# Recurrent gates as unsplit fp32 blocks in the quarters of the array, in a two-layer hybrid trunk

## The chip, the cores and the metric

The kernel is one program on one core of one Trainium2 chip. The metric is the device time of one execution in microseconds (us). Engines are named as in the profile: PE (TensorE matmul) and PEld (its weight loads), DVE (VectorE), ACT (ScalarE), POOL (GpSimd), SP (SyncE, which here issues all transfers).

## The reference

Two layers work on 1024 latent tokens and 256 context tokens, with 1024 features, in fp32. In each layer one input projection feeds two token mixers: attention, and a gated linear recurrence, which the change is about:

```python
def lru_coeffs(u, w_gates, b_gates, lam):            # for each direction d
    r = sigmoid(block_diag(u, w_gates[0]) + b_gates[0])   # 16 blocks of 64 x 64
    i = sigmoid(block_diag(u, w_gates[1]) + b_gates[1])
    log_a = -LRU_C * r * softplus(-lam)
    a = exp(log_a)
    b = sqrt(-expm1(2.0 * log_a)) * (i * u)
    return a, b
# h[t] = a[t] * h[t-1] + b[t], forward and backward, context before latent; y = h_fwd + h_bwd
# branch output: (y * silu(g_lru)) @ w_b_out
```

`u` is a slice of the projection after a centred depthwise convolution of width 4. Layer 1 needs no context outputs, so its branch gate is computed for the latent tokens alone.

## The kernel before

Features lie on the 128 partitions and tokens along the free axis, in three chunks: C (256 tokens), L0 and L1 (512 each). A projection tile is 128 output features: for each chunk 24 matmuls, since an fp32 product is made of three fp32r products of high and low parts (`gemm`, helper line L145). The high part of each weight half (`whi`, from `wraw`) is made on ACT (L226) or, where `weng[0]` is "g", on POOL (L224); the low part (`wlo`) on DVE (L227).

The recurrent stage comes after the q, k and v projections. It runs eight feature tiles t: a projection tile for `u` (evacuated by ACT into `up`), then one for the branch gate (`evac_g`: ACT takes a tanh from PSUM into `gbt`, DVE multiplies it with the same PSUM bank into `g2`, L876). When the last chunk of `u` is out, `conv` runs (one ACT, four DVE instructions), and DVE splits `uc` into `uh` and `ul`. The gate weights `gr` are block diagonal in a 128x128 square (two 64x64 blocks and zeros) and are split into `gh` (POOL) and `gl` (DVE). `gate` makes one gate of one chunk for one direction: three matmuls into one bank and an ACT tanh (L829) out of it, twelve times a tile. After the twelfth, `coeffs` puts out all that follows at once: per direction Exp, Tanh and Square on ACT (L844 to L846), two DVE products (L847, L848), Sqrt on ACT (L851), a POOL product (L853), the DVE scans in place over `ti` (L856; L858 and L860), and, per chunk, a POOL sum (L866), a DVE product with `g2` (L867) and the store `zb`.

What PE does, and in which order, is written out by hand: a list of events with due times in PE's planned time (`tl`); an event is run when the planned time of the matmuls put out so far passes it. For the other engines, the order of the program is a priority: an instruction takes its place in an engine's queue when its operands and buffers are ready in a planned run, and every queue then runs strictly in order. Nearly all tiles of the stage have a single buffer (`bufs=1`): `a1` of tile t+1 can't be written before the last reader of `a1` of tile t is done. PSUM has six banks under the tag "s" and two under "av"; projection chunks alternate between them, gates take "s". `mix` is a ring of four SBUF buffers shared by `up`, `c0` and `g2`.

After the eighth tile one more projection tile runs, then the events left over are drained, and attention begins with its loads of k, v and q, which stand behind the last `zb` stores on SP's queue.

Of the kernel before, what the change touches and what calls it, by code (L numbers as in the profile page):

```python
# [26 lines left out]
F32 = mybir.dt.float32  # L27
F32R = mybir.dt.float32r
AF = mybir.ActivationFunctionType
OP = mybir.AluOpType  # L30
# [6 lines left out]
CTX = 256  # L37
# [63 lines left out]
def trunk_kernel(ctx: ExitStack, tc: tile.TileContext, xT, cc, par, wmod, win, wgate, wo,  # L101
# [27 lines left out]
    def mix(name):  # L129
        return ring.tile([128, 1286], F32, name=name, tag="mix", bufs=4)  # L130
# [19 lines left out]


    par_sb = const.tile([128, DEPTH, PW], F32, name="par")
    DMA.dma_start(par_sb, par)
    cc_sb = const.tile([128, KT, 2], F32, name="cc")
    DMA.dma_start(cc_sb, cc)
    ones = const.tile([128, 1], F32, name="ones")
# [33 lines left out]


    sp4, hgb = {}, {}

    def recurrent_consts(l):
        lam = p(l, "lam", 0, 16)
# [513 lines left out]
    for l in range(DEPTH):  # L709
# [5 lines left out]
        with tc.tile_pool(name="qk", bufs=2, reuse_waits="tile") as work:  # L715
# [12 lines left out]
            def load_wv(i, k):  # L728
                wvr = sm("wvr")
                DMA.dma_start(wvr, win[l, V0 + i][:, 512 * k:512 * k + 512])  # L730
                cs_ = slice(i * 128, (i + 1) * 128)

                def f():
                    split(wvh[:, 4 * k:4 * k + 4, cs_], wvl[:, 4 * k:4 * k + 4, cs_],
                          wvr.rearrange("p (k n) -> p k n", k=4), "g", "v")
                tl.at(3.0, f)

            for i in range(2):
                for k in range(2):
                    tl.at(30.0 + 10.0 * (2 * i + k), lambda i=i, k=k: load_wv(i, k))  # L740
            tl.at(20.0, lambda: recurrent_consts(l))
            tl.fill(first)
            for g in groups[1:]:
# [26 lines left out]


        use_banks("g", "av")
        weng[0] = "g"
        with tc.tile_pool(name="lru", bufs=1, reuse_waits="tile") as work:
            sp = sp4[l]

            class Lru:
                def __init__(self, t):
                    self.t, self.left = t, len(ALL)
                    self.gr = work.tile([128, 4, 128], F32, name="gr", bufs=1)  # L780
                    DMA.dma_start(self.gr, wgate[l, t])
                    self.gh = work.tile([128, 4, 128], F32R, name="gh", bufs=2)
                    self.gl = work.tile([128, 4, 128], F32R, name="gl", bufs=2)
                    split(self.gh, self.gl, self.gr, "g", "v")
                    self.up = mix("up")
                    G.memset(self.up[:, 0:2], 0.0)
                    G.memset(self.up[:, 258:261], 0.0)
                    G.memset(self.up[:, 1285:1286], 0.0)
                    self.g2 = None
# [12 lines left out]
                def conv(self):  # L802
                    t, up = self.t, self.up
                    cw = [p(l, "conv_w", j * 8 + t) for j in range(4)]
                    c0 = mix("c0")[:, 0:1283]
                    S.activation(c0, up[:, 0:1283], AF.Identity, scale=cw[0], bias=p(l, "conv_b", t))
                    V.scalar_tensor_tensor(c0, up[:, 1:1284], cw[1], c0, op0=OP.mult, op1=OP.add)
                    V.scalar_tensor_tensor(c0, up[:, 2:1285], cw[2], c0, op0=OP.mult, op1=OP.add)
                    uc = self.uc = self.wt("uc", 2)
                    V.scalar_tensor_tensor(uc[:, 0:256], up[:, 3:259], cw[3], c0[:, 0:256],  # L810
                                           op0=OP.mult, op1=OP.add)
                    V.scalar_tensor_tensor(uc[:, 256:], up[:, 262:1286], cw[3], c0[:, 259:1283],
                                           op0=OP.mult, op1=OP.add)
                    self.uh, self.ul = self.wt("uh", dt=F32R), self.wt("ul", dt=F32R)
                    split(self.uh, self.ul, uc)
                    self.tg = [[self.wt(f"tr{d}"), self.wt(f"ti{d}")] for d in range(2)]
                    self.todo = [(d, gi, c) for d in range(2) for gi in range(2) for c in ("C", "L0", "L1")]
                    tl.at(28.0 if last else 36.0, self.gate)

                def gate(self):  # L820
                    d, gi, c = self.todo.pop(0)
                    dg = 2 * d + gi
                    off, n = CH[c]
                    ps = ptile("s", "gtps")
                    gh, gl, uh, ul = self.gh, self.gl, self.uh, self.ul
                    mm(ps[:, :n], gh[:, dg], uh[:, off:off + n], True, False)
                    mm(ps[:, :n], gh[:, dg], ul[:, off:off + n], False, False)
                    mm(ps[:, :n], gl[:, dg], uh[:, off:off + n], False, True)
                    S.activation(self.tg[d][gi][:, off:off + n], ps[:, :n], AF.Tanh, scale=0.5,  # L829
                                 bias=hgb[l][:, dg * 8 + self.t:dg * 8 + self.t + 1])  # L830
                    if self.todo:
                        tl.at(0.9, self.gate)
                    else:
                        self.coeffs()

                def coeffs(self):
                    t = self.t
                    co = []
                    for d in range(2):
                        s4 = sp[:, 0, d * 8 + t:d * 8 + t + 1]  # L840
                        s4n = sp[:, 1, d * 8 + t:d * 8 + t + 1]
                        tr_, ti = self.tg[d]
                        a, a2 = self.wt(f"a{d}"), self.wt(f"b{d}")
                        S.activation(a, tr_, AF.Exp, scale=s4n, bias=s4n)  # L844
                        S.activation(tr_, tr_, AF.Tanh, scale=s4, bias=s4)
                        S.activation(a2, a, AF.Square)  # L846
                        V.scalar_tensor_tensor(a2, a2, 1.0, tr_, op0=OP.add, op1=OP.mult)  # L847
                        V.scalar_tensor_tensor(ti, ti, 1.0, self.uc, op0=OP.add, op1=OP.mult)  # L848
                        co.append((a, a2, ti))
                    for a, a2, ti in co:  # L850
                        S.activation(a2, a2, AF.Sqrt, scale=0.25)  # L851
                    for d, (a, a2, ti) in enumerate(co):
                        G.tensor_mul(a2, a2, ti)  # L853
                        h = ti
                        if d == 0:
                            V.tensor_tensor_scan(h, a, a2, 0.0, op0=OP.mult, op1=OP.add)  # L856
                        else:
                            V.tensor_tensor_scan(h[:, 0:256][:, ::-1], a[:, 0:256][:, ::-1],  # L858
                                                 a2[:, 0:256][:, ::-1], 0.0, op0=OP.mult, op1=OP.add)
                            V.tensor_tensor_scan(h[:, 256:][:, ::-1], a[:, 256:][:, ::-1],  # L860
                                                 a2[:, 256:][:, ::-1], h[:, 0:1], op0=OP.mult, op1=OP.add)
                    for c in och:
                        off, n = CH[c]
                        y = self.g2[:, off:off + n]
                        s = co[0][2][:, off:off + n]
                        G.tensor_add(s, s, co[1][2][:, off:off + n])  # L866
                        V.scalar_tensor_tensor(y, s, 0.5, y, op0=OP.mult, op1=OP.mult)  # L867
                        DMA.dma_start(dd["zb"][t, c], y)

                def evac_g(self, c, ps):  # L870
                    off, n = CH[c]
                    if self.g2 is None:
                        self.g2 = mix("g2")
                    th = sm("gbt")
                    S.activation(th[:, :n], ps[:, :n], AF.Tanh, scale=0.5)
                    tl.at(0.9, lambda: V.scalar_tensor_tensor(  # L876
                        self.g2[:, off:off + n], th[:, :n], 1.0, ps[:, :n], op0=OP.add, op1=OP.mult))

            for t in range(8):
                u = Lru(t)  # L880
# [31 lines left out]


        use_banks("g")
        weng[0] = "a"
        with tc.tile_pool(name="att", bufs=2, reuse_waits="tile") as work:
            kv = {}

# [418 lines left out]
```

## Time and profile before

| | us |
|---|---|
| median of 3 runs (3193.29 to 3196.1) | 3194.48 |
| the profiled execution: its own time | 3197.96 |
| the profiled execution: span of the core | 3196.2 |
| recurrent stage of layer 0 (234 to 592): length, PE busy | 358, 343.6 |
| recurrent stage of layer 1 (1925 to 2250): length, PE busy | 325, 302.8 |
| granted PE clock, mean over the span | 0.986 |

The profile is that of one execution. "Busy" is the union of an engine's instructions. Matmuls overlap in their pipeline, so the duration of one (0.39 us) is longer than the distance from its start to the next one's start, and that distance is what it costs. An idle time is put down to the instruction that released the engine.

### The profile page before, as it was taken

The numbers are of one execution on the slowest core, as the hardware profiler recorded it, in microseconds if no ns is written. First come the engines' busy times: TensorE is split into PE (matmuls) and PEld (weight loads), VectorE is DVE, ScalarE is ACT, GpSimd is POOL, SyncE is SP. The second block draws the span as 40 slices with busy tenths as digits, with TensorE's granted clock in tenths as the row PEclk, the third lists the DMA queues.
The fourth block names the chain that finished last, engine by engine and source line by source line (L and its number), as shares of the span: only waits on it lengthen the run. The fifth ranks groups of instructions, "written<-read, shape, count | busy, mean of one in ns | idle before, by whom it ended". The sixth has DMA issues, their size and how long they took to land. (4 is left out here: it accounts for less than half of the span.)

```text
span 3196.2 us, 42921 instructions
## 1 busy us (share of the span) xinstructions
PE 3059.7 (96%) x14880; PEld 2430.8 (76%) x14880; DVE 2457.1 (77%) x3675; ACT 1749.6 (55%) x3060; POOL 1020.0 (32%) x777
## 2 busy tenths in 40 slices
PE   7999999999999999999899999899999999999999
PEld 3788788777777777787778778777777777777887
DVE  7665887589898988556685785997799999996544
ACT  4323667466666666545555324676477766673222
POOL 0211444234434333234432121433244444441000
PEclk9999999999999999999999999999999999999999
DMA  5443111311222122264555452111412121115554
GB/s 196 144 152 121 50 50 62 115 59 59 73 64 78 60 64 64 87 195 153 172 191 168 147 166 87 60 47 53 121 56 75 58 75 58 52 59 170 181 177 138
DMA packets 233049, 331.95 MB, mean 104 GB/s; under 512 B 53296, under 2 KB 99184, under 8 KB 232576
## 3 DMA queue, kind: packets, MB, share of 16 engines
q1 hardware_dynamic: 232832, 329.21, 32.0%
q8 instruction: 117, 1.92, 0.2%
q14 instruction: 100, 0.82, 0.1%
HBM read 252.54 MB, written 76.58 MB: 103 GB/s over the span
## 5 line engine op out<-in xcount | busy, mean ns | idle before, releaser
L145 PE MATMUL gps<-h,whi 128*128 128x512 f32 x3328 | 1041.4, 394 | 21.1 <-DVE g L876 15.3
L145 PEld LDWEIGHTS gps<-h,whi 128*128 128x128 f32 x3328 | 612.1, 190 | 148.4 <-issue 10.7
L1004 DVE TENSOR_TENSOR pl<-pf,ph 128x512 fp32r<-128x512 f32 x656 | 630.2, 961 | 83.1 <-ACT ph L1003 79.5
L145 PE MATMUL gps<-h,wlo 128*128 128x512 f32 x1664 | 654.5, 393 | 1.3 <-DVE wlo L227 1.3
L1002 ACT ACTIVATE pf<-s2ps 128x512 f32<-128x512 f32 x656 | 392.8, 599 | 348.1 <-issue 157.0
L1018 POOL TENSOR_TENSOR acc<-pf 128x512 f32<-128x512 f32 x256 | 352.0, 1375 | 713.1 <-ACT pf L1002 711.5
L980 DVE TENSOR_REDUCE mp<-s1ps 128x1 f32<-128x512 f32 (+1 forms) x800 | 454.1, 583 | 63.7 <-PE s1ps L145 60.8
L1003 ACT ACTIVATE ph<-s2ps 128x512 fp32r<-128x512 f32 x656 | 390.0, 595 | 0.0
L227 DVE TENSOR_TENSOR wlo<-wraw,whi 128x512 fp32r<-128x512 f32 x392 | 335.3, 878 | 61.4 <-ACT whi L226 32.7
L226 ACT ACTIVATE whi<-wraw 128x512 fp32r<-128x512 f32 x324 | 193.6, 627 | 333.8 <-PE gps L145 258.1
L145 PEld LDWEIGHTS gps<-h,wlo 128*128 128x128 f32 x1664 | 314.3, 189 | 69.9 <-DVE wlo L227 2.0
L145 PE MATMUL s1ps<-k,qa 128*128 128x512 f32 (+1 forms) x800 | 284.9, 363 | 12.3 <-DMA qa<-q0L 10.3
L145 PE MATMUL avps<-ph,vv 128*128 128x512 f32 x656 | 266.9, 407 | 0.0
L145 PE MATMUL avps<-pl,vv 128*128 128x512 f32 x656 | 260.2, 397 | 5.0 <-DVE pl L1004 4.9
L145 PE MATMUL s2ps<-qa,k 128*128 128x512 f32 x656 | 261.1, 398 | 1.8 <-DVE mp L980 1.6
L145 PE MATMUL s2ps<-qb,k 65*128 65x512 f32 x656 | 260.3, 397 | 0.0
L145 PE MATMUL gps<-e,whi 128*128 128x512 f32 x768 | 243.9, 399 | 0.2 <-DVE e L227 0.2
L360 POOL TENSOR_TENSOR macc<-macc,wmt 128x512 f32<-128x512 f32 x112 | 156.2, 1395 | 255.2 <-ACT wmt L358 221.9
L145 PE MATMUL qps<-h,whi 128*128 128x512 f32 x640 | 203.0, 398 | 1.5 <-DVE h L674 0.9
L1020 POOL TENSOR_TENSOR acc<-acc,pf 128x512 f32<-128x512 f32 x128 | 181.5, 1418 | 71.4 <-ACT pf L1002 69.2
L145 PE MATMUL gps<-c,whi 128*128 128x256 f32 x1024 | 197.2, 288 | 3.1 <-DVE c L222 2.1
L145 PEld LDWEIGHTS s1ps<-k,qa 128*128 128x128 f32 x800 | 151.6, 190 | 51.8 <-issue 6.4
(216 smaller groups left out, 5026.6 us busy)
## 6 DMA issues: line engine op xcount, KB each, us to landing
wraw<-in_win_dram SPq DMA_DIRECT2D x200, 256.0 KB
wraw<-in_wo_dram SPq DMA_DIRECT2D x192, 256.0 KB
wm<-in_wmod_dram SPq DMA_DIRECT2D x32, 512.0 KB
wm<-in_wmod_dram SPq DMA_DIRECT2D x8, 1024.0 KB
rb<-rq SPq DMA_DIRECT2D x64, 128.0 KB
k<-k SPq DMA_DIRECT2D x24, 320.0 KB
v<-vst SPq DMA_DIRECT2D x20, 256.0 KB
vv<-v SPq DMA_DIRECT2D x8, 640.0 KB
```

The source lines that it names most:

```text
L145: nc.tensor.matmul(o, a, b, start=start, stop=stop)
L226: S.activation(dst_hi, src, AF.Copy)
L227: (V if lo_eng == "v" else G).tensor_sub(dst_lo, src, r32(dst_hi))
L360: G.tensor_add(acc, acc, t)
L980: tl.at(0.3, lambda: V.reduce_max(self.mp[:, j, b:b + 1], ps[:, :n], axis=AX.X))
L1002: S.activation(pf, ps, AF.Exp)
L1003: S.activation(ph, ps, AF.Exp)
L1004: tl.at(1.4, lambda: V.tensor_sub(pl, pf, r32(ph)))
L1018: G.tensor_add(self.acc_tile(x), first, pf)
L1020: G.tensor_add(self.accs[x], self.accs[x], pf)
```

## The change

- The two 64x64 blocks of a gate tile are loaded unsplit (`gw`), without the zeros. Each gate of a chunk is made of two plain fp32 matmuls with 64 rows and 64 columns. Direction 0 puts block h on the partitions of half h, direction 1 on those of the other half, so the four matmuls of one gate of both directions use the four quarters of the array and write two banks. `gate` makes all four gates of a chunk in one visit (eight matmuls, four banks, four tanh), three visits a tile.
- Everything of direction 1 therefore stands with the two halves of the partitions swapped. `exchange` (two transfers, SBUF to SBUF) makes a swapped copy `us` of `uc`, and swaps the result of the backward scan back, into `a1`, before the sum. The parameters of direction 1 are loaded swapped (`recurrent_params`, five small transfers).
- `uh`, `ul`, `gh`, `gl` and their splits are gone. The first gate is due 24 (layer 1: 20) after the convolution instead of 36 (28).
- `coeffs` is cut into thirteen events with due times, direction 1 first; the merge is due 4 after the exchange.
- `evac_g`: ACT takes both the tanh and a copy out of PSUM (`th`, `g2`); one DVE product per tile joins them later, from SBUF.
- `weng[0]` stays "a": in the recurrent stage the high parts of weights are made on ACT instead of POOL. `c0` has a buffer of its own.

```diff
+    def recurrent_params():
+        DMA.dma_start(par_sb[:, :, lam_c:lam_c + 8], par[:, :, lam_c:lam_c + 8])
+        for a, n in ((gate_c + 16, 16), (lam_c + 8, 8)):
+            for h in range(2):
+                DMA.dma_start(par_sb[64 * h:64 * h + 64, :, a:a + n], par[64 - 64 * h:128 - 64 * h, :, a:a + n])
...
-        weng[0] = "g"
...
-                    split(self.gh, self.gl, self.gr, "g", "v")
+                    self.gw = work.tile([128, 4, 64], F32, name="gw", bufs=2)
+                    for h in (slice(0, 64), slice(64, 128)):
+                        DMA.dma_start(self.gw[h], wgate[l, t][h, :, h])
...
-                    c0 = mix("c0")[:, 0:1283]
+                    c0 = work.tile([128, 1283], F32, name="c0", tag="c0")
...
-                    split(self.uh, self.ul, uc)
+                    self.us = self.exchange(uc, self.wt("us"))
...
-                    tl.at(28.0 if last else 36.0, self.gate)
+                    self.todo = ["C", "L0", "L1"]
+                    tl.at(20.0 if last else 24.0, self.gate)
+
+                def exchange(self, a, b):
+                    DMA.dma_start(b[0:64], a[64:128])
+                    DMA.dma_start(b[64:128], a[0:64])
+                    return b
...
-                    mm(ps[:, :n], gh[:, dg], uh[:, off:off + n], True, False)
-                    mm(ps[:, :n], gh[:, dg], ul[:, off:off + n], False, False)
-                    mm(ps[:, :n], gl[:, dg], uh[:, off:off + n], False, True)
...
+                    ps = [ptile("s", "gtps") for _ in range(4)]
+                    for gi in range(2):
+                        for h in range(2):
+                            rows = slice(64 * h, 64 * h + 64)
+                            for d in range(2):
+                                o = 64 * (h ^ d)
+                                mm(ps[2 * gi + d][o:o + 64, :n], self.gw[rows, 2 * d + gi], self.uc[rows, off:off + n],
+                                   True, True, 0.03 + 0.245 * n / 512)
+                    for gi in range(2):
+                        for d in range(2):
+                            dg = 2 * d + gi
+                            S.activation(self.tg[d][gi][:, off:off + n], ps[2 * gi + d][:, :n], AF.Tanh, scale=0.5,
+                                         bias=hgb[l][:, dg * 8 + self.t:dg * 8 + self.t + 1])
                     if self.todo:
-                        tl.at(0.9, self.gate)
+                        tl.at(3.6, self.gate)
                     else:
-                        self.coeffs()
+                        tl.at(0.5, self.coeffs)
...
+                    for at, fn, *d in ((0, decay, 1), (0.5, gated, 1), (2, gated, 0), (4.5, decay, 0), (5, square, 1),
+                                       (9.5, square, 0), (11, root), (14, product, 1), (17, product, 0),
+                                       (17.5, scan, 1), (21.5, scan, 0), (22, self.exchange, i1, a1), (26, merge)):
+                        tl.at(at, lambda fn=fn, d=d: fn(*d))
...
-                    th = sm("gbt")
-                    S.activation(th[:, :n], ps[:, :n], AF.Tanh, scale=0.5)
-                    tl.at(0.9, lambda: V.scalar_tensor_tensor(
-                        self.g2[:, off:off + n], th[:, :n], 1.0, ps[:, :n], op0=OP.add, op1=OP.mult))
+                        self.g2, self.th = mix("g2"), self.wt("th")
+                    g2, th = self.g2, self.th
+                    S.activation(th[:, off:off + n], ps[:, :n], AF.Tanh, scale=0.5)
+                    S.activation(g2[:, off:off + n], ps[:, :n], AF.Copy)
+                    if c == och[-1]:
+                        a = 0 if "C" in och else CTX
+                        tl.at(2.5, lambda: V.scalar_tensor_tensor(g2[:, a:TOK], th[:, a:], 1.0, g2[:, a:TOK],
+                                                                  op0=OP.add, op1=OP.mult))
...
```

In the events, `decay` is Exp, Tanh and Square of one direction, `gated` and `square` the two DVE products, `root` both Sqrt, `product` the POOL product, `scan` the scan (two for direction 1), `merge` the sums, the products with `g2` and the stores.

## Rows read from the trace of the kernel before

**Rows 1.** The page: busy time of each engine, and the chain's shares by engine.
```profile
PE 3059.7 (96%) x14880; PEld 2430.8 (76%) x14880; DVE 2457.1 (77%) x3675; ACT 1749.6 (55%) x3060; POOL 1020.0 (32%) x777
PE 31%; DVE 7%; issue 3%; ACT 1%; POOL 1%; DMA 0%; SPq 0%; DVEq 0%; POOLq 0%; ACTq 0%
```

**Rows 2.** Windows: one tile's period of layer 0, then the sum of six of layer 1.
```profile
core 0: us, PE busy (x) PEld busy (x) DVE busy (x) ACT busy (x) POOL busy (x), PEclk, DMA share, GB/s
446.10:482.80 36.70, 35.14 (x182) 29.84 (x181) 30.93 (x25) 26.20 (x31) 17.47 (x14) 1.00 0.16 54
...
sum 205.40, PE 187.63 PEld 155.67 DVE 188.98 ACT 140.75 POOL 82.33; mean PE 31.27 PEld 25.94 DVE 31.50 ACT 23.46 POOL 13.72
```

**Rows 3.** TensorE's waits, us in total, times, longest: layer 0, then layer 1.
```profile
PE gps L145 <- DVE g L876: 7.9, 7, 2.1
PE gtps L145 <- ACT ti L829: 4.8, 3, 3.0
...
PE gtps L145 <- DVE g L876: 11.7, 3, 5.2
PE gps L145 <- DVE g L876: 7.4, 4, 2.9
```

**Rows 4.** Timeline of TensorE: two matmuls of a gate.
```profile
start us, us, engine line op out<-in xcount [idle before <-releaser]
446.30 0.39 PE L145 MATMUL gtps<-uh,gl 128*128 128x512 f32 x1
446.53 0.40 PE L145 MATMUL gtps<-uh,gh 128*128 128x512 f32 x1
```

**Rows 5.** Same columns: the softmax sums (lps) between other matmuls.
```profile
2303.64 0.28 PE L145 MATMUL s1ps<-k,qa 128*128 128x256 f32 x1
2303.85 1.06 PE L145 MATMUL lps<-acc,ones 128*32 128x512 f32 x8
2305.18 0.39 PE L145 MATMUL avps<-pl,vv 128*128 128x512 f32 x1
```

**Rows 6.** Groups of instructions, shapes kept apart: busy us, mean ns, idle before.
```profile
L226 ACT ACTIVATE whi<-wraw 128x512 fp32r<-128x512 f32 x324 | 193.6, 627 | 333.8 <-PE gps L145 258.1 <-issue 35.5 <-PE qps L145 19.4
L145 PE MATMUL lps<-acc,ones 128*32 128x512 f32 x544 | 76.6, 604 | 9.6 <-DVE mp L980 9.4
L829 ACT ACTIVATE tr<-gtps,hgb 128x512 f32<-128x512 f32 x64 | 42.8, 696 | 13.1 <-PE gtps L145 13.0
L227 DVE TENSOR_TENSOR ul<-uc,uh 128x1280 fp32r<-128x1280 f32 x16 | 24.1, 1508 | 0.0
L227 DVE TENSOR_TENSOR gl<-gr,gh 128x512 fp32r<-128x512 f32 x16 | 23.6, 1474 | 17.5 <-POOL gh L224 17.5
L875 ACT ACTIVATE gbt<-gps 128x512 f32<-128x512 f32 x32 | 18.8, 597 | 18.8 <-PE gps L145 18.7
L222 DVE CAST uh<-uc 128x1280 fp32r<-128x1280 f32 x16 | 16.1, 1006 | 0.1
```

**Rows 7.** Timelines: coefficients of a layer 1 tile; last, a scan of layer 0.
```profile
2071.87 0.47 ACT L829 ACTIVATE ti<-gtps,hgb 128x256 f32<-128x256 f32 x1 [3.03 <-DVE g L867]
2088.10 2.45 ACT L851 ACTIVATE b<-b 128x1280 f32<-128x1280 f32 x2
...
2090.58 6.75 POOL L853 TENSOR_TENSOR b<-b,ti 128x1280 f32<-128x1280 f32 x2
...
2094.43 5.58 DVE L856 TENSOR_TENSOR_SCAN ti<-a,b 128x1280 f32<-128x1280 f32 x1
2104.44 2.79 DVE L867 SCALAR_TENSOR_TENSOR g<-ti,g 128x512 f32<-128x512 f32 x2 [0.89 <-POOL ti L866]
...
428.55 3.23 DVE L856 TENSOR_TENSOR_SCAN ti<-a,b 128x1280 f32<-128x1280 f32 x1
```

**Rows 8.** Timeline of SyncE and ScalarE: a weight load and who waits for it.
```profile
585.93 0.33 SPq L261 DMA_DIRECT2D wraw<-in_win_dram  x1
...
588.47 0.63 ACT L226 ACTIVATE whi<-wraw 128x512 fp32r<-128x512 f32 x1 [0.98 <-DMA wraw<-in_win_dram]
```

More of the change, by code (lines that the diff above doesn't have):

```diff
@@ L152, in trunk_kernel @@
     par_sb = const.tile([128, DEPTH, PW], F32, name="par")
-    DMA.dma_start(par_sb, par)
+    gate_c, lam_c = PC["gate_b"][0], PC["lam"][0]
+    DMA.dma_start(par_sb[:, :, 0:gate_c + 16], par[:, :, 0:gate_c + 16])
     cc_sb = const.tile([128, KT, 2], F32, name="cc")
@@ L740, in trunk_kernel @@
                     tl.at(30.0 + 10.0 * (2 * i + k), lambda i=i, k=k: load_wv(i, k))
+            if l == 0:
+                tl.at(10.0, recurrent_params)
             tl.at(20.0, lambda: recurrent_consts(l))
@@ L779, in __init__ @@
                     self.t, self.left = t, len(ALL)
[L780 to L783, printed above, removed]
-                    split(self.gh, self.gl, self.gr, "g", "v")
+                    self.gw = work.tile([128, 4, 64], F32, name="gw", bufs=2)
+                    for h in (slice(0, 64), slice(64, 128)):
+                        DMA.dma_start(self.gw[h], wgate[l, t][h, :, h])
                     self.up = mix("up")
@@ L813, in conv @@
                                            op0=OP.mult, op1=OP.add)
-                    self.uh, self.ul = self.wt("uh", dt=F32R), self.wt("ul", dt=F32R)
-                    split(self.uh, self.ul, uc)
+                    self.us = self.exchange(uc, self.wt("us"))
                     self.tg = [[self.wt(f"tr{d}"), self.wt(f"ti{d}")] for d in range(2)]
-                    self.todo = [(d, gi, c) for d in range(2) for gi in range(2) for c in ("C", "L0", "L1")]
-                    tl.at(28.0 if last else 36.0, self.gate)
+                    self.todo = ["C", "L0", "L1"]
@@ L820, in gate @@
+                    tl.at(20.0 if last else 24.0, self.gate)
[3 more added lines that the diff above has]
+                    return b
                 def gate(self):
-                    d, gi, c = self.todo.pop(0)
-                    dg = 2 * d + gi
+                    c = self.todo.pop(0)
                     off, n = CH[c]
-                    ps = ptile("s", "gtps")
-                    gh, gl, uh, ul = self.gh, self.gl, self.uh, self.ul
@@ L826, in gate @@
-                    mm(ps[:, :n], gh[:, dg], uh[:, off:off + n], True, False)
-                    mm(ps[:, :n], gh[:, dg], ul[:, off:off + n], False, False)
-                    mm(ps[:, :n], gl[:, dg], uh[:, off:off + n], False, True)
-                    S.activation(self.tg[d][gi][:, off:off + n], ps[:, :n], AF.Tanh, scale=0.5,
-                                 bias=hgb[l][:, dg * 8 + self.t:dg * 8 + self.t + 1])
+                    ps = [ptile("s", "gtps") for _ in range(4)]
[6 more added lines that the diff above has]
+                                   True, True, 0.03 + 0.245 * n / 512)
@@ L836, in coeffs, with decay @@
                 def coeffs(self):
                     t = self.t
-                    co = []
-                    for d in range(2):
+                    (a0, b0, i0), (a1, b1, i1) = co = [(self.wt(f"a{d}"), self.wt(f"b{d}"), self.tg[d][1]) for d in range(2)]
+                    def decay(d):
+                        a, b, _ = co[d]
+                        tr_ = self.tg[d][0]
                         s4 = sp[:, 0, d * 8 + t:d * 8 + t + 1]
                         s4n = sp[:, 1, d * 8 + t:d * 8 + t + 1]
-                        tr_, ti = self.tg[d]
-                        a, a2 = self.wt(f"a{d}"), self.wt(f"b{d}")
@@ L844, in coeffs @@
                         S.activation(a, tr_, AF.Exp, scale=s4n, bias=s4n)
                         S.activation(tr_, tr_, AF.Tanh, scale=s4, bias=s4)
[L846 to L851, printed above, removed]
@@ L852, in coeffs, with gated, square @@
-                    for d, (a, a2, ti) in enumerate(co):
-                        G.tensor_mul(a2, a2, ti)
-                        h = ti
+                        S.activation(b, a, AF.Square)
+                    def gated(d):
+                        i = co[d][2]
+                        V.scalar_tensor_tensor(i, i, 1.0, self.us if d else self.uc, op0=OP.add, op1=OP.mult)
+                    def square(d):
+                        b = co[d][1]
+                        V.scalar_tensor_tensor(b, b, 1.0, self.tg[d][0], op0=OP.add, op1=OP.mult)
@@ L855, in coeffs, with root, product, scan @@
+                    def root():
+                        for d in range(2):
+                            S.activation(co[d][1], co[d][1], AF.Sqrt, scale=0.25)
+                    def product(d):
+                        G.tensor_mul(co[d][1], co[d][1], co[d][2])
+                    def scan(d):
+                        a, b, h = co[d]
                         if d == 0:
-                            V.tensor_tensor_scan(h, a, a2, 0.0, op0=OP.mult, op1=OP.add)
+                            V.tensor_tensor_scan(h, a, b, 0.0, op0=OP.mult, op1=OP.add)
@@ L857, in coeffs @@
                         else:
                             V.tensor_tensor_scan(h[:, 0:256][:, ::-1], a[:, 0:256][:, ::-1],
-                                                 a2[:, 0:256][:, ::-1], 0.0, op0=OP.mult, op1=OP.add)
+                                                 b[:, 0:256][:, ::-1], 0.0, op0=OP.mult, op1=OP.add)
                             V.tensor_tensor_scan(h[:, 256:][:, ::-1], a[:, 256:][:, ::-1],
-                                                 a2[:, 256:][:, ::-1], h[:, 0:1], op0=OP.mult, op1=OP.add)
@@ L862, in coeffs @@
[L862 to L868, printed above, removed]
+                                                 b[:, 256:][:, ::-1], h[:, 0:1], op0=OP.mult, op1=OP.add)
@@ new lines, in merge @@
+                    def merge():
+                        for c in och:
+                            off, n = CH[c]
+                            y = self.g2[:, off:off + n]
+                            s = i0[:, off:off + n]
+                            G.tensor_add(s, s, a1[:, off:off + n])
+                            V.scalar_tensor_tensor(y, s, 0.5, y, op0=OP.mult, op1=OP.mult)
+                            DMA.dma_start(dd["zb"][t, c], y)
+                    for at, fn, *d in ((0, decay, 1), (0.5, gated, 1), (2, gated, 0), (4.5, decay, 0), (5, square, 1),
+                                       (9.5, square, 0), (11, root), (14, product, 1), (17, product, 0),
+                                       (17.5, scan, 1), (21.5, scan, 0), (22, self.exchange, i1, a1), (26, merge)):
+                        tl.at(at, lambda fn=fn, d=d: fn(*d))
@@ L872, in evac_g @@
                     if self.g2 is None:
-                        self.g2 = mix("g2")
-                    th = sm("gbt")
-                    S.activation(th[:, :n], ps[:, :n], AF.Tanh, scale=0.5)
-                    tl.at(0.9, lambda: V.scalar_tensor_tensor(
-                        self.g2[:, off:off + n], th[:, :n], 1.0, ps[:, :n], op0=OP.add, op1=OP.mult))
+                        self.g2, self.th = mix("g2"), self.wt("th")
[6 more added lines that the diff above has]
+                                                                  op0=OP.add, op1=OP.mult))
             for t in range(8):
@@ L914, in trunk_kernel @@
         use_banks("g")
-        weng[0] = "a"
         with tc.tile_pool(name="att", bufs=2, reuse_waits="tile") as work:
```

## The prediction

> **What bounds the kernel now.** I read the page first, then the windows of the recurrent stage, then PE's waits there, then the timelines of single tiles. On the page PE is busy in 3059.7 of 3196.2 us and leads the chain that ended last [rows 1]; no other engine comes near, so time is won where PE does less or waits less. The change touches only the two recurrent stages. There a tile of layer 0 takes 36.70 us, of which PE is busy 35.14, and one of layer 1 takes 205.40 / 6 = 34.23 us with 31.27 busy [rows 2]. So PE idles 1.56 and 2.96 us a tile, 8 x 1.56 + 8 x 2.96 = 36 us in all. The waits say why: gates and projection chunks stand still until DVE's product of the branch gate (L876) gives a PSUM bank back, 7.9 + 11.7 + 7.4 = 27 us, because that product is queued behind DVE's scans; 4.8 us more go to a gate's tanh [rows 3].
>
> There is a second clock behind this one. In layer 1 the first `ti` tanh of a tile begins at 2071.87, after a wait of 3.03 us for DVE's last product of the tile before (L867), since `ti` has one buffer; the same product of this tile ends at 2104.44 + 2.79 = 2107.23 [rows 7]. The loop from merge to merge is thus 35.4 us here, as long as the tile. It is made of 18.7 us until both Sqrt are done (2088.10 + 2.45), 3.9 until the scan starts, 5.6 of forward scan, and 7.2 for the backward scan and the merge [rows 7].
>
> **The gates on PE.** Before, 12 gates of three matmuls: 24 of 512 columns and 12 of 256. Two starts are 0.23 us apart at 512 [rows 4]; at 256 I take half. That is 24 x 0.23 + 12 x 0.115 = 6.9 us a tile. After, each visit is two rounds of four fp32 matmuls. The nearest row is the softmax sum: four fp32 matmuls of 512 columns in four strips of 32 columns, shown as 8 instructions of 604 ns [rows 5, 6]. A single pass of 512 columns lasts 0.39 [rows 4], so each of the 8 holds two passes (0.39 + 0.23 = 0.62); one after another they would need 16 x 0.23 = 3.7 us. But from the matmul ahead (2303.64) to the second one behind (2305.18) only 1.54 us go by; less 0.115 and 0.23 for the two neighbours, the four cost 1.19, of which 4 x 0.23 = 0.92 is the streaming of one and 0.27 the way in and out [rows 5]. So four strips run side by side. If four quarters do too, a visit of 512 costs 0.27 + 2 x 0.92 = 2.11, the visit of 256 costs 0.27 + 2 x 0.46 = 1.19, and a tile 5.4 instead of 6.9: 1.5 us saved, 24 us over 16 tiles. No row shows two row halves at work at once; the bounds are four at a time (5.4) and two at a time (twice the streaming: 0.27 x 3 + 2 x 4.6 = 10.0). I take four: the sums are the same data type and the same pattern of short matmuls into one bank.
>
> The Trainium skill speaks against this: "TensorEngine Tiling (Array Packing)", Restrictions and Gotchas, says that tiles of different rows can't reach the same PSUM bank at once, and here both row halves of one direction write one bank, on different partitions. By that rule the tile costs 10.0 and not 5.4. The sums above all read full rows, so no row here bears on it.
>
> **The floor.** With 1.5 less, PE's own time is 33.6 a tile in layer 0 and 29.8 in layer 1. Were all waits gone too, the stages would lose 8 x (36.7 - 33.6) + 8 x (34.2 - 29.8) = 60 us.
>
> **ScalarE.** It gains a copy beside each tanh of the branch gate (0.6 a chunk: 1.2, with context 1.6) and four weight splits of 0.63 (2.5) [rows 6]. Its 26.2 of 36.7 and 23.5 of 34.2 [rows 2] become 30.3 of about 34 and 27.2 of about 32, 85 to 89%. It is not the bound, but a bank now waits behind whatever stands in its queue: a group of Exp, Tanh, Square (some 4 us) or both Sqrt. Projection chunks last 24 x 0.23 = 5.5 us and alternate between eight banks, so they can bear that. A visit takes four of the six "s" banks, and its tanh need 4 x 0.7 = 2.8 us [rows 6], against 3.6 planned to the next visit; a miss stops PE for 1 or 2 us.
>
> The Trainium skill, "TensorEngine Tiling (Array Packing)", Performance Considerations, advises the opposite of the change, both ScalarE and VectorE for emptying PSUM once tiling speeds PE up. By it ScalarE would become the bound, which is the last rival below.
>
> **VectorE and GpSimd.** DVE loses 1.0 + 1.5 + 1.5 us a tile [rows 6] of 31 [rows 2]; the branch gate's product costs it as much as before, but no bank hangs on it any more. POOL loses four weight splits and `gh`. Both are slack on the floor; what counts is that the L876 wait goes (27 us at most).
>
> **The loop after.** Direction 1's chain is now: three `ti` tanh (2), Exp, Tanh and Square of both directions with one evacuation among them (8 + 1), a table load and both Sqrt (1.3 + 2.5), about 15 us; the product 3.4 (half of 6.75); the scan 3.3 with POOL still, up to 5.6 beside it (3.23 against 5.58) [rows 7]; the exchange; the merge about 4.1 (two sums and 2.79). No row has an SBUF-to-SBUF transfer. A weight load of 256 KB, issued at 585.93, lets ACT start at 588.47, 2.5 us later [rows 8]; the exchange is 640 KB in two, so between 2.5 and 2.5 x 2.5 = 6.3, and I take 5. Sum: 15 + 3.4 + 3.3 to 5.6 + 5 + 4.1 = 31 to 33 us. The early gate (12 or 8 planned us sooner) and events with due times keep scans from standing ahead of weight splits, but don't shorten this loop. So layer 1, with PE at 29.8, is held near 32; layer 0, with PE at 33.6, near 34.
>
> The exchange also waits in SP's queue for the scan, and behind it stand weight loads and `zb` stores. A weight tile is loaded a tile ahead (over 11 us), so a few us of that are covered; without this cover every us late would be one of PE's.
>
> **Costs of nothing.** The swap of `uc` (5 us) has 20 planned us before anything reads `us`. Five small parameter transfers run while the q products do, with SP free; uncovered they are under 2 us, once. The last tile's chain, on which attention's first loads wait, gains the exchange (2.5 to 6.3) and starts earlier, since only two visits (2 x 2.1) stand after the last fill and not twelve gates (6.9); I take 0.
>
> **Sum.** 8 x (36.7 - 34.0) + 8 x (34.2 - 32.0) = 22 + 18 = 39 us off the profiled 3197.96, which lies 3.5 above the median: 3194.5 - 39 = 3155.
>
> **Rivals.** (a) The loop doesn't matter and PE runs at its floor: 60 us less, 3134. For it: half of the loop can start before the merge (direction 0's Exp to Square need neither `ti` nor `a1`). (b) The loop is as long as before, because the exchange and ScalarE's fuller queue eat what the splits gave: layer 1 gains nothing, layer 0 between 0 and 2 us a tile, so 3178 to 3195. For it: the 3.03 us wait of [rows 7] is already a loop wait, and the changed loop has a new link of 5 us. (c) The quarters run in pairs: PE's own time becomes 35.14 + 3.1 = 38.2 and 31.27 + 3.1 = 34.4; with 0.5 of waits left, 8 x 2.0 + 8 x 0.7 = 22 us more, 3216. It is slower from about 8.5 us of gates a tile, 1.6 above the old 6.9, where layer 0's idle time is used up. (d) ScalarE is late: if each of three visits lost 2 us to a bank, a tile would be 33.6 + 6 = 39.6 and 35.8, 36 us more, 3230; slower from about 1.2 us a visit.
>
> **Chances.** Forecast (3140 to 3172) 0.50; (a) 0.14; (b) 0.18, of which 0.08 within 0.2% (6.4 us, about what this kernel's measurement can tell from no change); (c) 0.13; (d) 0.05. Faster 0.50 + 0.14 + 0.10 = 0.74, same 0.08, slower 0.18. The range reaches from 3128 (a little past PE's floor) to 3205, short of (c) and (d), which hold 0.18.
>
> **What would show it.** Starts on PE: a visit of 512 takes 2.1 us (right) or 4 (c). No PE wait on DVE `g` in these stages. Tile periods from the `zb` stores of 34 and 32; if 33.6 and 29.8, (a). ScalarE's `ti` tanh or Exp waiting for DVE's merge means the loop binds, and its length says whether by the exchange: from the scan's end to the first POOL sum, 5 us. PE waits on ACT `ti` or `tr` beyond 1 us a visit mean (d). I would be wrong above all if row halves exclude one another, or if the exchange takes over 10 us.

## The result, and the profile after

| | before | after |
|---|---|---|
| median of 4 runs each, us | 3195.29 (3193.29 to 3199.36) | 3219.61 (3215.15 to 3220.80) |
| ratio, 95% interval | | 1.0072 [1.0054, 1.0089] |
| profiled execution: span, mean granted clock | 3196.2, 0.986 | 3217.6, 0.977 |

The changed kernel is slower by 24 us. I had forecast 39 us less, with a range that ended at 3205. From here on "before" and "after" name the two kernels. In the code of after, the gates' tanh are L847, `decay` is L864 to L866, both Sqrt L878, the POOL product L881, the scans L886 to L890, the merge L898 (POOL sum) and L899 (DVE product), the branch gate's product L917, its evacuations L913 and L914.

First the page and the chain's shares, which answer to [rows 1]: PE is busy for all but the same time, and it still leads the chain. That isn't the same work: in experiment 1 below the same 15072 matmul instructions keep PE busy for 3024.0 us.

```profile
PE 3062.5 (95%) x15072; PEld 2362.0 (73%) x15072; DVE 2365.3 (74%) x3603; ACT 1794.1 (56%) x3168; POOL 934.5 (29%) x693
...
PE 25%; DVE 4%; ACT 1%; issue 1%; DMA 1%; POOL 0%; SPq 0%; DVEq 0%; POOLq 0%; ACTq 0%
```

The windows of the recurrent stages, with the columns of [rows 2]: the sum over four tiles of layer 0, then one tile of layer 1 and the sum over six.

```profile
sum 154.20, PE 143.53 PEld 104.29 DVE 101.03 ACT 111.46 POOL 45.12; mean PE 35.88 PEld 26.07 DVE 25.26 ACT 27.86 POOL 11.28
...
2117.50:2155.60 38.10, 33.94 (x173) 22.95 (x173) 24.99 (x19) 26.41 (x35) 8.50 (x7) 0.90 0.28 80
...
sum 225.30, PE 198.08 PEld 137.70 DVE 148.86 ACT 163.25 POOL 55.00; mean PE 33.01 PEld 22.95 DVE 24.81 ACT 27.21 POOL 9.17
```

A tile now lasts 154.20 / 4 = 38.6 us in layer 0 (36.70 in the one tile of [rows 2]) and 225.30 / 6 = 37.6 in layer 1 (34.23). PE idles 4.5 us a tile in layer 1, and its granted clock in the tile shown is 0.90. Layer 0 ends only 3 us late (its last `zb` store at 590.79 against 587.63), since its first merge comes 14 us sooner (323.49 against 337.58); the other 19 us, up to the last store of layer 1, are lost after that.

PE's waits, which answer to [rows 3], layer 0 and then layer 1:

```profile
PE gtps L145 <- ACT ti L847: 19.5, 7, 4.3
PE gps L145 <- DVE wlo L235: 8.3, 1, 8.3
...
PE gtps L145 <- ACT ti L847: 32.8, 11, 4.5
```

The waits for DVE's branch gate product, 27 us of [rows 3], are gone. Gates now wait for their own evacuation, 19.5 + 32.8 = 52 us. ScalarE's waits in layer 1 say what that evacuation waits for:

```profile
ACT ti L847 <- DVE g L899: 33.6, 7, 6.9
ACT ti L847 <- DVE g L917: 28.0, 4, 7.9
```

So a `ti` tanh waits for the merge of the tile before (L899), or for something put down to L917. The timeline of one tile, from the end of one merge to the end of the next, answers to [rows 7]; first ScalarE, then POOL, DVE and the exchange on SP's queue.

```profile
2117.62 0.84 ACT L847 ACTIVATE ti<-gtps,hgb 128x256 f32<-128x256 f32 x2 [6.90 <-DVE g L899]
2118.34 1.27 ACT L847 ACTIVATE tr<-gtps,hgb 128x512 f32<-128x512 f32 x2
...
2126.47 2.82 ACT L864 ACTIVATE a<-tr,sp 128x1280 f32<-128x1280 f32 x2
...
2136.58 2.44 ACT L878 ACTIVATE b<-b 128x1280 f32<-128x1280 f32 x2
...
2151.91 0.47 ACT L847 ACTIVATE ti<-gtps,hgb 128x256 f32<-128x256 f32 x1 [6.69 <-DVE g L917]
2155.63 0.47 ACT L847 ACTIVATE ti<-gtps,hgb 128x256 f32<-128x256 f32 x1 [3.25 <-DVE g L899]
...
2138.00 5.86 POOL L881 TENSOR_TENSOR b<-b,ti 128x1280 f32<-128x1280 f32 x2 [18.11 <-ACT b L878]
2151.97 2.48 POOL L898 TENSOR_TENSOR ti<-ti,a 128x512 f32<-128x512 f32 x2 [8.11 <-DVE g L917]
...
2140.99 3.41 DVE L888 TENSOR_TENSOR_SCAN ti<-a,b 128x256 f32<-128x256 f32 x1 [5.17 <-POOL b L881]
2144.44 2.35 DVE L890 TENSOR_TENSOR_SCAN ti<-a,ti,b 128x1024 f32<-128x1024 f32 x1
2150.61 1.22 DVE L917 SCALAR_TENSOR_TENSOR g<-th,g 128x1024 f32<-128x1024 f32 x1
2153.26 2.34 DVE L899 SCALAR_TENSOR_TENSOR g<-ti,g 128x512 f32<-128x512 f32 x2 [1.44 <-POOL ti L898]
...
2146.93 0.46 SPq L828 DMA_DIRECT2D a<-ti  x1
2147.44 0.60 SPq L829 DMA_DIRECT2D a<-ti  x1
```

ScalarE stands still for 6.90 us in front of two tanh, until the merge ends. The eight tanh of the other two visits, two weight splits, an evacuation and the convolution's part stand behind them in its queue, and Exp begins only at 2126.47, 8.85 us later. At 2151.91 and 2155.63 it stands still twice again, 6.69 + 3.25 us: one `ti` is held by the exchange that reads it, the other by the merge. The first of these is put down to L917, which had ended at 2151.83 by chance; POOL's sum, which does need the exchange, starts at the same moment (2151.97).

### The profile page after: what moved, and what is told of

Its sections match the earlier page's. It is cut to its first block, busy times and chain, and to the rows that moved or that the text cites. A ratio compares the mean times of both kernels' runs of the same rounds, so it can differ in the third digit from the quotient of the medians.

```text
span 3217.6 us, 43400 instructions
## 1 busy us (share of the span) xinstructions
PE 3062.5 (95%) x15072; PEld 2362.0 (73%) x15072; DVE 2365.3 (74%) x3603; ACT 1794.1 (56%) x3168; POOL 934.5 (29%) x693
## 5 line engine op out<-in xcount | busy, mean ns | idle before, releaser
L234 ACT ACTIVATE whi<-wraw 128x512 fp32r<-128x512 f32 x392 | 234.3, 628 | 332.6 <-PE gps L145 269.4
L235 DVE TENSOR_TENSOR wlo<-wraw,whi 128x512 fp32r<-128x512 f32 x392 | 300.3, 786 | 109.8 <-ACT whi L234 109.3
L881 POOL TENSOR_TENSOR b<-b,ti 128x1280 f32<-128x1280 f32 x32 | 102.8, 3224 | 335.8 <-ACT b L878 335.8
```

The source lines that it names most:

```text
L881: G.tensor_mul(co[d][1], co[d][1], co[d][2])
```

## The experiments

Their theories: the loop through the single buffer of `ti` sets the tile's period (L); the exchange is what makes it long (X); ScalarE's load does (S); the quarters exclude one another (Q). Each ratio is to the kernel before, on the same chip.

**1. Both scans write over `b`.** The last reader of `ti` is then the POOL product, and the loop is cut.

```diff
-                        a, b, h = co[d]
+                        a, b, _ = co[d]
+                        h = b
...
-(22, self.exchange, i1, a1)
+(22, self.exchange, b1, a1)
...
-                            s = i0[:, off:off + n]
+                            s = b0[:, off:off + n]
```

> The changed kernel, but the scans write in place over b instead of over ti, so ti is free after the product and not after the merge; nothing else differs. Loop theory (ti's single buffer makes the next tile's tanh, and all that stands behind it in ScalarE's queue, wait for the merge): the tile periods fall from 38.6 and 37.6 us to about 34 and 32, time 3140 to 3165 us, and the waits of ACT ti on DVE's merge vanish. Rival, the exchange's 5 us of transfer are the cost in themselves: 3210 to 3225. Rival, ScalarE has too much work: 3210 to 3225.

3133.90 us, ratio 0.9805 [0.9789, 0.9821]: 85 us below after by the ratios, (1.0072 - 0.9805) x 3194, and below the 3140 to 3165 of L. The windows of two tiles of layer 1:

```profile
2001.10:2031.10 30.00, 30.00 (x169) 22.28 (x168) 23.11 (x17) 25.81 (x33) 8.55 (x7) 1.00 0.32 87
2031.10:2060.60 29.50, 29.50 (x167) 21.70 (x166) 24.57 (x20) 28.10 (x38) 9.96 (x7) 1.00 0.36 103
```

In these two tiles PE is busy all the time, at a clock of 1.00; in both stages together it has two waits of over 2 us left, 9.1 for a weight's low part in layer 0 and 5.7 for a `tr` tanh in layer 1. This is the floor: my rival (a) said 29.8 us a tile and 3134. ScalarE is as busy as it was (25.81 and 28.10 us, against a mean of 27.21), so S falls too. This version beats both kernels.

**2. Without the swap back.** This kernel leaves out the second exchange; its sum takes direction 1's scan with the halves still swapped, another result.

```diff
-(21.5, scan, 0), (22, self.exchange, i1, a1), (26, merge)
+(21.5, scan, 0), (26, merge)
...
-                            G.tensor_add(s, s, a1[:, off:off + n])
+                            G.tensor_add(s, s, i1[:, off:off + n])
```

> The changed kernel without the transfer that swaps the backward scan's result back: the sum takes the unswapped result, so half of the sum stands on the wrong partitions; all other work stays. Loop theory: the loop is 5 us shorter, 33 us, so PE's own 33.5 decides in layer 0 and the loop in layer 1: 3140 to 3160 us. ScalarE's load as the cause: within 10 us of 3220.

3233.19 us, ratio 1.0120 [1.0105, 1.0135]: slower than after, so X falls, and so does my expectation. The stores of `zb` in layer 1 are (2240.85 - 2013.13) / 6 = 37.95 us apart. The timeline of ScalarE, then of DVE:

```profile
2128.25 0.84 ACT L847 ACTIVATE ti<-gtps,hgb 128x256 f32<-128x256 f32 x2 [7.94 <-DVE g L899]
...
2157.35 2.80 DVE L886 TENSOR_TENSOR_SCAN ti<-a,b 128x1280 f32<-128x1280 f32 x1
2160.06 2.33 DVE L235 TENSOR_TENSOR wlo<-wraw,whi 128x512 fp32r<-128x512 f32 x2
2162.32 2.28 DVE L917 SCALAR_TENSOR_TENSOR g<-th,g 128x1024 f32<-128x1024 f32 x1
2164.52 0.68 DVE L899 SCALAR_TENSOR_TENSOR g<-ti,g 128x512 f32<-128x512 f32 x1
```

The 5 us of the exchange had lain beside the other direction's scan (2.80) and work that DVE has to do anyway (2.33 and 2.28). Without it these stand ahead of the merge by themselves. And the `ti` that the exchange had let go at its landing is now held until POOL's sums end (in layer 1 ScalarE waits 25.2 us for them, in three waits). That it is 15 us slower than after, and not just as slow, I put down to this; it wasn't tried by itself.

**3. The weight splits back on POOL.** `weng[0] = "g"` in the recurrent stage again, "a" after it.

> The changed kernel with the weight splits of the recurrent stage on GpSimd again. If ScalarE's added work is the cause, 2.5 us a tile come back: 3180 us or less. Loop theory: two of the four splits lie in the loop (1.3 us a tile, 20 us in all at most), and GpSimd beside the scans makes these longer again: 3200 to 3222.

3230.69 us, ratio 1.0114 [1.0095, 1.0133]. Relief for ScalarE gains nothing, against S; it even lies above the 3200 to 3222 of L, and why wasn't tried. In this trace ScalarE's waits are put down to the transfer itself (`ACT ti L848 <- DMA a<-ti`, 52.5 us in 7 waits; L848 is L847 there), which bears out the reading of L917 above.

**4. to 6. Parts of the change in the kernel before.** In 4, ACT also copies the branch gate out of PSUM:

```diff
                     S.activation(th[:, :n], ps[:, :n], AF.Tanh, scale=0.5)
+                    S.activation(self.g2[:, off:off + n], ps[:, :n], AF.Copy)
                     tl.at(0.9, lambda: V.scalar_tensor_tensor(
-                        self.g2[:, off:off + n], th[:, :n], 1.0, ps[:, :n], op0=OP.add, op1=OP.mult))
+                        self.g2[:, off:off + n], th[:, :n], 1.0, self.g2[:, off:off + n], op0=OP.add, op1=OP.mult))
```

In 5 the scans of before write over `a2` (`h = a2`, and the sums read it), and 6 is both.

> The kernel before with one part of the change: ScalarE copies the branch gate out of PSUM too, and DVE's product reads the copy. If the 27 us in which PE waits for that product's bank were a cost of their own, 3168 us. If the loop from merge to merge was the bound already, the waits only move to another place: 3185 to 3198.

> The kernel before with the one edit of the first experiment: the scans write over a2 (the buffer of b) and not over ti. If the loop through ti was a bound there too, layer 1 gains most of its idle 2.96 us a tile and layer 0 less, 3170 to 3185 us; the waits for the branch gate's bank stay. If those waits alone were the cost of the kernel before: 3188 to 3197.

> The kernel before with ScalarE's copy of the branch gate and the scans over a2. If loop and bank waits are all that keeps PE from its own pace there, 36 us less, 3155 to 3165 us, and the rest of the way to the first experiment's 3134 is what the quarters save on PE (24 us by the prediction). If the two edits take the same time away, no better than the better one of them.

| | us | ratio |
|---|---|---|
| 4 | 3178.67 | 0.9950 [0.9935, 0.9965] |
| 5 | 3188.64 | 0.9983 [0.9970, 0.9996] |
| 6 | 3165.36 | 0.9912 [0.9896, 0.9929] |

The evacuation alone is worth 0.50%, some 16 us of the 27 that I had put on those waits; run 4 lies between my two expectations. Run 5 misses its expectation: the loop of before, which I had read as a second clock from the 3.03 us in [rows 7], was worth 0.17% [0.04, 0.30], some 5 us. In the next tile of that trace the same tanh began without a wait:

```profile
2108.39 0.47 ACT L829 ACTIVATE ti<-gtps,hgb 128x256 f32<-128x256 f32 x1
```

In all 16 tiles of before there are six such waits, 22.8 us. With the branch gate out of the way the loop costs more: 6 is 0.38% below 4, some 12 us.

From 6 to experiment 1 the ratios leave 34 us, give or take 7. The two profiled executions are 27.5 us apart, and PE's busy time makes 26.6 of that (3050.6 against 3024.0), near the 24 that I expected of the quarters.

**7. Two quarters at a time.** Experiment 1 with both directions in the same half of the columns: `o = 64 * h`, no exchange at all, direction 1's parameters unswapped, and 0.49 in place of 0.245 as the planned cost.

> The first experiment's kernel with both directions on the diagonal quarters: no half is swapped, no exchange, parameters as they are, but only two quarters can work at once (the planned cost of a gate matmul is doubled with it). By the prediction's rounds a visit of 512 takes 0.27 + 4 x 0.92 = 3.9 us and a tile 10.0 instead of 5.4, on PE's own time: 16 x 4.6 = 73 us more than 3134, 3195 to 3215. If four quarters did not run side by side in the changed kernel, this costs PE nothing more and saves the exchange: 3125 to 3140.

3179.78 us, ratio 0.9951 [0.9936, 0.9966], 47 us above experiment 1 by the ratios and below the 3195 to 3215 that I expected. The timelines of PE, first after (a visit of 256 and one of 512 columns), then this kernel (one of 256, then two of 512 together):

```profile
284.37 0.39 PE L145 MATMUL gps<-h,wlo 128*128 128x512 f32 x1
284.68 1.09 PE L145 MATMUL gtps<-uc,gw 64*64 64x256 f32 x16
...
286.28 0.39 PE L145 MATMUL gps<-h,wlo 128*128 128x512 f32 x1
...
287.65 0.39 PE L145 MATMUL gps<-h,wlo 128*128 128x512 f32 x1
287.97 1.95 PE L145 MATMUL gtps<-uc,gw 64*64 64x512 f32 x16
...
290.42 0.39 PE L145 MATMUL gps<-h,wlo 128*128 128x512 f32 x1
```

```profile
428.46 0.39 PE L145 MATMUL gps<-h,wlo 128*128 128x512 f32 x1
428.77 1.99 PE L145 MATMUL gtps<-uc,gw 64*64 64x256 f32 x16
...
431.27 0.39 PE L145 MATMUL gps<-h,wlo 128*128 128x512 f32 x1
...
432.28 7.13 PE L145 MATMUL gtps<-uc,gw 64*64 64x512 f32 x32
439.35 0.73 PE L145 MATMUL gps<-h,whi 128*128 128x512 f32 x2
```

From a `wlo` matmul ahead of a visit to the first one behind it there are three ordinary starts, 3 x 0.23. So in after a visit of 256 costs 286.28 - 284.37 - 0.69 = 1.22, and one of 512 costs 290.42 - 287.65 - 0.69 = 2.08: 1.22 + 2 x 2.08 = 5.4 a tile. In pairs the visit of 256 costs 431.27 - 428.46 - 0.69 = 2.12, and the two of 512 last 439.35 - 432.28 = 7.07. All four quarters of after do run side by side, against Q. PE is busy 57.5 us longer than in experiment 1 (3081.5 against 3024.0), near the 16 x (9.2 - 5.4) = 61 of these visits, but it idles 13 us less, so the span is only 44 us longer.

**8. Gates later.** After with due times 32 and 28 in place of 24 and 20, near those of before.

> The changed kernel with the first gate due 8 planned us later (32 and 28 after the convolution), nothing else. Buffer theory: ScalarE no longer stands still in front of the first ti tanh, but the loop through ti stays, so 3195 to 3220 us. If the early due time is the fault in itself: 3170 or less.

3272.46 us, ratio 1.0237 [1.0222, 1.0252]: a miss, 53 us above after. The first merge is 18.3 us later than in after (341.82 against 323.49). And the loop is longer, with another queue order on DVE: the stores of `zb` in layer 1 are (2287.78 - 2046.43) / 6 = 40.2 us apart.

```profile
2147.57 5.54 DVE L886 TENSOR_TENSOR_SCAN ti<-a,b 128x1280 f32<-128x1280 f32 x1 [3.87 <-POOL b L881]
...
2162.63 1.73 DVE L899 SCALAR_TENSOR_TENSOR g<-ti,g 128x512 f32<-128x512 f32 x1 [5.36 <-POOL ti L898]
2164.29 1.54 DVE L814 SCALAR_TENSOR_TENSOR c<-up,par,c 128x1283 f32<-128x1283 f32 x1
2165.76 0.68 DVE L899 SCALAR_TENSOR_TENSOR g<-ti,g 128x512 f32<-128x512 f32 x1
```

The forward scan is first, so nothing lies beside the exchange but 1.27 us of weight split (DVE idles 5.36), and the next tile's convolution stands between the two halves of the merge. The length of the loop hangs on what stands in its queues.

**9. Only the forward scan over `b`.** As experiment 1, for direction 0 alone.

> The changed kernel with only the forward scan over b: ti of direction 0 is free after its product, ti of direction 1 still until the swap back has landed. If each ti buffer closes a loop of its own, the loop is now that from landing to landing, shorter by the merge (3.7 us), 34.4 us a tile: about 3160 us (3150 to 3175). If the forward buffer alone mattered: 3130 to 3140.

3156.86 us, ratio 0.9896 [0.9877, 0.9915]: the time is as expected. The tile is not quite: the stores of `zb` in layer 1 are (2164.48 - 1970.92) / 6 = 32.3 us apart, where I had said 34.4; that is between 37.6 and the 30.1 of experiment 1, where they are (2150.07 - 1969.55) / 6 apart. The `ti` that the exchange reads still holds ScalarE up, 29.2 us in 4 waits. Either half of the loop costs.

**10. All events put out at once.** Experiment 1 with `fn(*d)` in place of `tl.at(at, ...)`, in the same order.

> The first experiment's kernel (scans over b) with all events of the coefficients put out at once after the last gate, in the same order, as the kernel before did. If spreading them over time keeps scans from standing ahead of weight splits on DVE, this loses 5 to 20 us: 3139 to 3155. If the freed buffer is all that matters: 3128 to 3139.

3212.38 us, ratio 1.0069 [1.0050, 1.0087]: a miss, 84 us above experiment 1. PE's waits of layer 0 and layer 1, ScalarE's of layer 1, and SP's queue:

```profile
PE gps L145 <- DVE wlo L235: 37.6, 4, 9.7
...
PE gps L145 <- DVE wlo L235: 29.6, 4, 9.8
...
ACT whi L234 <- DMA wraw<-in_win_dram: 38.4, 5, 8.9
...
2161.99 0.50 SPq L828 DMA_DIRECT2D a<-b  x1
...
2166.71 2.41 SPq L269 DMA_DIRECT2D wraw<-in_win_dram  x2
...
2169.35 0.63 ACT L234 ACTIVATE whi<-wraw 128x512 fp32r<-128x512 f32 x1 [8.82 <-DMA wraw<-in_win_dram]
```

A weight load is now issued behind the exchange, which waits for the scan; ScalarE waits 8.82 us for it and PE for ScalarE and DVE. I read these waits so that SP's order is the whole of it, and not scans ahead of weight splits on DVE, as I had expected; neither was tried by itself.

**11. DVE takes the branch gate's product out of PSUM again.** Experiment 1 with `evac_g` of before.

> The first experiment's kernel with the branch gate emptied as in the kernel before: DVE's product reads PSUM, no copy on ScalarE. If the bank waits come back behind DVE's scans, as the 15 us that the copy alone gave before say: 3140 to 3152. If ScalarE's relief is worth more: 3125 to 3134.

3166.08 us, ratio 0.9926 [0.9908, 0.9945], 39 us above experiment 1 by the ratios: the direction was right, the size more than expected. PE waits for that product for 13.6 us in layer 0 and 19.6 in layer 1, in four waits each.

**12. Both exchanges issued by GpSimd.** Experiment 1 with `G.dma_start` in `exchange`.

> The first experiment's kernel with both exchanges issued from GpSimd's queue, which is idle two thirds of the stage, instead of SyncE's. If weight loads behind the exchange in SyncE's queue cost the 8 to 9 us wait for wlo at the end of layer 0's stage: 3124 to 3131. If issuing costs GpSimd as much or the wait has another cause: 3132 to 3150.

3135.14 us, ratio 0.9831 [0.9809, 0.9853]; the intervals of 1 and 12 overlap. PE's wait for a weight's low part in layer 0 is still there (8.5 us), so it has another cause. With the events spread out, the exchange in SP's queue costs nothing that shows.

## Why the prediction was wrong, step by step

**The gates on PE: right.** 2.11, 1.19 and 5.4 us were forecast; 2.08, 1.22 and 5.4 came. The time is near the 3216 of rival (c), but it has nothing to do with it. The rule of the Trainium skill that I weighed ("TensorEngine Tiling (Array Packing)", Restrictions and Gotchas, no common bank for tiles of different rows) would have made it 10.0. The trace doesn't agree: here both row halves write one bank, on different partitions, at the full rate of four, and only the layout of experiment 7, which uses two quarters, costs 2.12 + 7.07 = 9.2.

**The branch gate: right.** No PE wait on DVE's product is left. By the sign that I gave for rival (d), over 1 us a visit of waits for ScalarE, (d) would be met: 52 us over 48 visits. But ScalarE alone is not late: it is busy 27.9 of 38.6 and 27.2 of 37.6 us, and at the floor, without those waits, 53.91 of 59.50. The advice of the same page of the Trainium skill (Performance Considerations, both engines for emptying PSUM) is not borne out here, where DVE's queue holds the scans: with DVE in it again, experiment 11 loses 39 us.

**The loop after: the step that failed, in its first term.** I had "three `ti` tanh (2), Exp, Tanh and Square of both directions with one evacuation among them (8 + 1), a table load and both Sqrt (1.3 + 2.5), about 15 us". The measured pieces are these:

| from the end of a merge | forecast | measured |
|---|---|---|
| until Exp | 2 | 8.85 (2117.62 to 2126.47) |
| Exp to both Sqrt done | 12.8 | 12.6 (to 2139.02) |
| until the scan starts | 3.4 | 2.0 |
| backward scan | 3.3 to 5.6 | 5.8 (to 2146.79) |
| exchange | 5 | 5.1 (to 2151.91) |
| merge | 4.1 | 3.7 (to 2155.63) |
| sum | 31 to 33 | 38.0 |

I had counted the three `ti` tanh that wait, as if the others had been done before them. But a visit holds the tanh of all four gates, so the very first visit already has both `ti` in it, and ScalarE's queue is in order: ten of the twelve tanh, two splits, an evacuation and the convolution's part all come after the merge. A row that I had read could have told me: before needs 18.7 us from its first `ti` tanh until both Sqrt are done, and I put about 15 on the same stretch of a queue to which the change adds work. It takes 21.4.

The forecast that the loop would bind was right for layer 1; in layer 0, where I had put PE's own 33.6 ahead of it, the tile went to 38.6 as well. The exchange, the term I was least sure of, was right. The loop was 5 to 7 us longer than I said, and with it the tile of layer 1, and that turned a gain into a loss. Rival (b), which named ScalarE's fuller queue, comes nearest, but it had the loop no longer than before (35.4).

The scan's term came out at its upper end, and one of its rows was misread: the 3.23 us "with POOL still" are none, since POOL was at two weight splits then.

```profile
428.04 4.14 POOL L224 TENSOR_SCALAR whi<-wraw 128x512 fp32r<-128x512 f32 x2
```

Alone the scan takes 2.80 (2146.71 above).

**What the loop costs in full.** Experiment 1 removes it and gets 85 us back. My floor (rival a) came out to the microsecond, which is partly luck: up to the last `zb` store, experiment 1 is 31 us ahead of before in layer 0 and gains 31 more in layer 1, where the floor had 25 and 35. The argument that I gave for that rival, that half of the loop can start before the merge, was what failed in the kernel as it is. Experiment 9, where one half of the loop is cut, lands on 3156.86, close to my number by luck, since it isn't the kernel that I forecast. In before I had the loop "as long as the tile", and took that for a second bound; experiment 5 shows that it cost about 5 us there, and 4 and 6 that it cost some 12 once the bank waits were gone.

**A term that I didn't have: PE's clock.** In layer 1 the tile lasts 37.6 and PE's idle time is 4.5, so 33.0 are busy, 3.2 more than the floor of 29.8. The windows of after around the waits show where most of it comes from (the clock is the column behind POOL):

```profile
2140.00:2148.80 8.80, 8.80 (x68) 6.47 (x70) 7.77 (x3) 4.16 (x9) 3.86 (x2) 1.00 0.09 19
2148.80:2152.40 3.60, 2.21 (x14) 1.05 (x6) 3.02 (x4) 0.47 (x1) 0.43 (x1) 1.00 0.81 236
2152.40:2156.20 3.80, 1.11 (x5) 0.23 (x5) 2.34 (x2) 0.57 (x2) 2.05 (x2) 0.66 0.21 78
2156.20:2160.90 4.70, 4.70 (x18) 1.91 (x19) 0.00 (x0) 4.67 (x7) 0.16 (x3) 0.55 0.22 83
2160.90:2170.00 9.10, 9.10 (x42) 7.54 (x41) 6.32 (x5) 9.10 (x11) 0.00 (x0) 1.00 0.07 16
```

PE is busy 2.21 + 1.11 of 7.40 us; the clock falls in the second of these stretches, is 0.55 for the next 4.7 us of full work, near the lower level of 1.2 GHz, and is back at 1.00, 2.4 GHz, after that. At 0.55 these 4.7 us do the work of 2.6, so about 2.1 us are lost behind this one stall (an estimate from that row). In the two tiles of experiment 1, where PE never stops, the clock is 1.00. Over the whole execution PE is busy for 38.5 us more in after than in experiment 1, with the same matmuls, at a mean clock of 0.977 against 0.986. How much of that lengthens the tile isn't shown: as long as the loop sets the tile's length, slower matmuls may only fill time in which PE would stand idle.

**Left open.** Whether the slower gates after a stall lengthen the loop itself wasn't tried; the row that would show it is small (a `ti` tanh waits 0.55 us for PE). What the due times alone are worth, with the exchange on another queue, wasn't tried either.

## What to carry to other kernels

When a buffer with one copy closes a loop from tile to tile, count all that stands in the in-order queue behind the first instruction that needs the buffer, not the instruction alone: here 2 us were 8.85. Then look for a buffer that is dead at that point: writing the scan over its own input turned a loss of 24 us into a gain of 61. What a loop costs depends on what else holds the tile, too: the same edit was worth some 5 us in before. A new link in the loop is not its price either: the 5 us of the exchange lay beside other work, and taking out the swap back made the kernel slower.

## What the runs showed of the hardware that I had not expected

- Four fp32 matmuls of 64 rows and 64 columns run at once in the array's quarters, two row halves into one PSUM bank: 2.08 us for two rounds of 512 columns, against 7.07 / 2 = 3.54 in two quarters.
- Two stalls of PE of 1.43 and 2.65 us close together were followed by 4.7 us at a clock of 0.55, about 2 us (an estimate) on top of 4.1.
- By these rows a DVE scan gets nowhere while POOL's product runs. The backward scan of 256 columns took 3.41 us beside it, but ended only 0.54 after it (2144.40 against 2143.86), and takes 0.66 behind it (experiment 8, 2153.04). The forward scan of before ended 2.68 after the product (2100.01 against 2097.33, [rows 7]), that of experiment 8 2.67 after it, and alone it takes 2.80. So the scan isn't slowed down: it stands until the product ends.
- A swap of 640 KB inside SBUF took 5.0 us from its issue at 2146.93 to the first reader at 2151.91.
